# A decoder block in float32 halves on one core: low parts of the MLP's first weights, and two block sums of its second weights, made by accumulating DMA

## The chip, the cores and the metric

The kernel runs on one core of a Trainium2 chip. Time is device time in microseconds (us), from launch to end. The engines are named as in the profile: PE multiplies matrices, PEld loads its stationary operand, DVE and ACT work element by element, POOL is the general engine (GpSimd), and SP issues most DMAs. A DMA moves data between the chip's memory (HBM) and SBUF; PSUM holds the results of PE.

## The reference

One decoder block over 512 tokens of width 1024, all in float32. Only the MLP matters here:

```python
h = rms_norm(x, mlp_norm_g[i])
x = x + jnp.square(jax.nn.relu(h @ w_ff1[i])) @ w_ff2[i]
```

Here `w_ff1` is 1024 x 4096 and `w_ff2` is 4096 x 1024. In front of it stand an attention branch, a recurrent branch and their merge (`w_out`); behind it a gate with embeddings (`w_ple_gate`, `w_ple_proj`) and a last norm.

## The kernel before

**Products in halves.** Each float32 operand is split in a high part, rounded to the type fp32r, and a low part, the rest. A product is then three matmuls: high by high, high by low, low by high (`mm3`, L186, and `rows3`, L201). All weights come in units of 128 x 1024 float32 (512 KB) in `wts`. The list `seq` (L127) names the units in the order in which they are used.

**The flow of a unit.** `load_to` (L156) starts the plain load of a unit into one of two `w_raw` buffers on SP's queue. `fetch_to` (L164) then makes the parts in one of three pairs of buffers: ACT copies with rounding to `w_hi` (L175), and DVE subtracts that from the raw values to give `w_lo` (L176). `weights` (L179) hands the pair to the product. During the third step of a unit's product, `step` (L196) lets the second next unit be fetched; since there are three pairs, that fetch can't start before the unit ahead of the running one is done.

**The MLP** (from L1081). The hidden columns are taken in four groups (`qd`) of 1024. In a group, eight units of `w_ff1` (`U_FF1`) give eight tiles of 128 hidden columns by 512 tokens, 24 matmuls each. `squared` (L1126) applies ReLU and square and makes parts and sums of these tiles: `fA11`, `fA2`, `fS3`, `fS`. The second product works on 2 x 2 blocks with seven block products instead of eight (Strassen's way, in Winograd's form). The left blocks are the tiles of `squared` (`LEFT`, L1092). The right blocks are B11, B21, B12 and B22 of the group's `w_ff2`, each in two units (a, b), and sums of them. `load_block` (L1149) loads a block; `sums_early` (L1155), `T1` (L1161) and `T4` (L1164) form the sums on DVE: B12 becomes B22 - B12, T2 is that plus B11, B11 becomes B22 - T2, B21 becomes B21 - T2. `RIGHT` (L1167) names the right block of each of the seven products, `BEFORE` (L1168) the sum that is formed ahead of a unit, and `LOADS` (L1176) which blocks are loaded beside which unit of the first product. Each block is split like other weights, by `fetch_to`, since `load_to` leaves out `U_FF2`. `seventh` (L1178) runs one block product, two units of 12 matmuls each; `to_x` (L1189) adds finished sums to the residual stream `xs`.

**The order of the queues.** Each engine runs its queue in order. The framework's planner orders the queues when the program is built: by the order of the program, but what it expects to be ready may pass what it expects to wait. So the blocks of a group are loaded while the second product of the group before runs, as soon as their buffers are free, though they stand behind it in the program.

**Around it.** Ahead of the MLP `embeddings` (L1031) and `gained` (L1016) make the transposed input `hx`, `norm_of` (L1038) the norm with the scratch tile `sqj`, and `spread` (L1109) brings the norm to all partitions.

Of the kernel before, what the change touches and what calls it, by code (L numbers as in the profile page):

```python
# [10 lines left out]
F32 = mybir.dt.float32  # L11
F32R = mybir.dt.float32r
BF16 = mybir.dt.bfloat16
AF = mybir.ActivationFunctionType
ALU = mybir.AluOpType
# [3 lines left out]
P = 128  # L19
T = 512  # L20
D = 1024
# [19 lines left out]
U_PLE, U_QKV, U_RW, U_GSB, U_GRW, U_UPSB, U_UPRW, U_OUT, U_FF1, U_FF2, U_GATE = range(11)  # L41
UNITS = {U_PLE: 2, U_QKV: 12, U_RW: 14, U_GSB: 8, U_GRW: 8, U_UPSB: 4, U_UPRW: 4, U_OUT: 8, U_FF1: 32, U_FF2: 32, U_GATE: 8}
UBASE = {}
# [42 lines left out]
def tile_block(ctx: ExitStack, tc: tile.TileContext, xT, xt, pT, wts, lora, cols_d, gfin_d, consts_d, out, dbg=None):  # L86
    nc = tc.nc
    act, dve, pool, pe, sync = nc.scalar, nc.vector, nc.gpsimd, nc.tensor, nc.sync
# [3 lines left out]
    def r32(ap):  # L92
        return ap.bitcast(F32)
# [33 lines left out]
    seq = []  # L127
# [25 lines left out]
    def unit(i):  # L153
        return wts[UBASE[seq[i][0]] + seq[i][1]]

    def load_to(n):  # L156
        while len(loaded) < min(n, len(seq)):
            i = len(loaded)
            loaded.append(None)
            if seq[i][0] != U_FF2:  # L160
                loaded[i] = wpool.tile([P, 1024], F32, name="w_raw", bufs=2)
                sync.dma_start(out=loaded[i], in_=unit(i))

    def fetch_to(n, ahead=0):  # L164
        while state["i"] < min(n, len(seq)):
            i = state["i"]
            state["i"] += 1
            load_to(i + 1 + ahead)
            raw = loaded[i] if seq[i][0] != U_FF2 else sources[seq[i]]()
            if seq[i] in homes:  # L170
                hi, lo = homes[seq[i]]()
            else:
                hi = wpool.tile([P, 1024], F32R, name="w_hi")
                lo = wpool.tile([P, 1024], F32R, name="w_lo")
            act.copy(out=hi, in_=raw)  # L175
            dve.tensor_tensor(out=lo, in0=raw, in1=r32(hi), op=ALU.subtract)  # L176
            ready.setdefault(seq[i], []).append((hi, lo))

    def weights(*u):  # L179
        assert seq[state["used"]] == u, (seq[state["used"]], u)  # L180
        state["used"] += 1
        fetch_to(state["used"])
        state["due"] = 3
        return ready[u].pop(0)
# [35 lines left out]
    def split(hi, lo, src):  # L220
        act.copy(out=hi, in_=src)  # L221
        dve.tensor_tensor(out=lo, in0=src, in1=r32(hi), op=ALU.subtract)
# [13 lines left out]
    def root(r, n, v):  # L236

        vi, ri = v.bitcast(mybir.dt.int32), r.bitcast(mybir.dt.int32)
        dve.tensor_scalar(out=ri, in0=vi, scalar1=1, scalar2=None, op0=ALU.logical_shift_right)
        dve.tensor_scalar(out=ri, in0=ri, scalar1=-1.0, scalar2=float(0x5f3759df), op0=ALU.mult, op1=ALU.add)  # L240
        for _ in range(3):
            dve.tensor_tensor(out=n, in0=r, in1=r, op=ALU.mult)
            dve.scalar_tensor_tensor(out=n, in0=n, scalar=-0.5, in1=v, op0=ALU.mult, op1=ALU.mult)
            dve.scalar_tensor_tensor(out=r, in0=n, scalar=1.5, in1=r, op0=ALU.add, op1=ALU.mult)
# [27 lines left out]
    with ExitStack() as sA:  # L272
# [43 lines left out]
        with ExitStack() as s1:  # L316
# [205 lines left out]
            pss = [psm.tile([P, T], F32, name="ps_m") for _ in range(2)]  # L522
# [4 lines left out]
            for _ in islice(v, 1):  # L527
# [6 lines left out]
                              op0=ALU.mult, op1=ALU.add)  # L534
# [37 lines left out]
        with ExitStack() as s2:  # L572
# [39 lines left out]
            for hp in range(HP):  # L612
                csl = slice(hp * P, (hp + 1) * P)
                for i, (name, got) in enumerate((("w0", cum_), ("a0", a_all))):
# [3 lines left out]
                    t = p2.tile([P, T], F32, name=name, bufs=HP)  # L618
# [388 lines left out]
    def by_token(u, i, rhs, half):  # L1007

        pss = [ps_main() for _ in range(TT)]
        for kk in range(4):  # L1010
            w = weights(u, i + half * 4 + kk)
            for tt in range(TT):
                rows3(pss[tt], w, rhs, tt, kk * 2, kk == 0, kk == 3)
        return pss
# [23 lines left out]
    def norm_of(pool_, name):  # L1038

        st = pool_.tile([P, 3, TT], F32, name=name)  # L1040
        sq = pool_.tile([P, D], F32, name="sqj", tag="T2a")
        for tt in range(TT):
            act.activation(out=sq, in_=xs[:, tt, :], func=AF.Square, accum_out=st[:, 0, tt:tt + 1])
        dve.tensor_scalar(out=st[:, 0, :], in0=st[:, 0, :], scalar1=1.0 / D, scalar2=NORM_EPS, op0=ALU.mult, op1=ALU.add)
        root(st[:, 1, :], st[:, 2, :], st[:, 0, :])
        return st[:, 1, :]

    with ExitStack() as s3:
# [23 lines left out]
        for half in range(2):  # L1072
            pss = by_token(U_OUT, 0, mg, half)
# [8 lines left out]
    p4 = sM.enter_context(tc.tile_pool(name="p4", bufs=1))  # L1082
    HT = T // 2
# [13 lines left out]
    def kept(tt):  # L1097
        t = p4.tile([P, 512], F32, name="pl", tag="rk", bufs=4)
        return t

    for half in range(2):
        for tt in (half * 2, half * 2 + 1):
            t = kept(tt)
# [14 lines left out]
    def minus(out, a, b):  # L1118
        dve.tensor_tensor(out=out, in0=a, in1=b, op=ALU.subtract)  # L1119

    def plus(out, a, b):
        dve.tensor_tensor(out=out, in0=a, in1=b, op=ALU.add)

    lower = {}

    def squared(ps, m):  # L1126
        if m < 4:
            r = lower[m] = p4.tile([P, T], F32, name="rk", bufs=4)
        else:
            r = p4.tile([P, T], F32, name="r")  # L1130
        dve.scalar_tensor_tensor(out=r, in0=ps, scalar=0.0, in1=rs2, op0=ALU.max, op1=ALU.mult)
        act.activation(out=r, in_=r, func=AF.Square)
        sums = const.tile([P, 4, HT], F32, name="sums", tag="lora_w")
        lo_, hi_ = r[:, 0:HT], r[:, HT:T]
        if m < 4:
            split(fA11[0][:, m], fA11[1][:, m], lo_)
            minus(sums[:, 0], lo_, hi_)
            split(fS3[0][:, m], fS3[1][:, m], sums[:, 0])
        else:
            k, low = m - 4, lower[m - 4]  # L1140
            split(fA2[0][:, k], fA2[1][:, k], r.rearrange("p (j t) -> p j t", j=2))
            plus(sums[:, 1], low[:, HT:T], hi_)
            minus(sums[:, 2], sums[:, 1], low[:, 0:HT])
            minus(sums[:, 3], lo_, sums[:, 2])
            split(fS[0][:, k], fS[1][:, k], sums[:, 1:4])

    blocks = {}

    def load_block(qd, n, p_):  # L1149

        i = {"B11": 0, "B21": 2, "B12": 4, "B22": 6}[n] + p_
        t = blocks[n, p_] = p4.tile([P, 1024], F32, name=f"{n}{'ab'[p_]}")
        sync.dma_start(out=t, in_=wts[UBASE[U_FF2] + qd * 8 + i])

    def sums_early(p_):  # L1155

        minus(blocks["B12", p_], blocks["B22", p_], blocks["B12", p_])
        blocks["T2", p_] = p4.tile([P, 1024], F32, name=f"T2{'ab'[p_]}")
        plus(blocks["T2", p_], blocks["B12", p_], blocks["B11", p_])

    def T1(p_):  # L1161
        minus(blocks["B11", p_], blocks["B22", p_], blocks["T2", p_])

    def T4(p_):  # L1164
        minus(blocks["B21", p_], blocks["B21", p_], blocks["T2", p_])

    RIGHT = ("B11", "B21", "T2", "B11", "B12", "B22", "B21")  # L1167
    BEFORE = {4: lambda: T1(0), 5: lambda: T1(1), 7: lambda: T4(0), 8: lambda: T4(1)}  # L1168
    for qd in range(4):
        for i in range(7):  # L1170
            for p_ in range(2):
                def source(i=i, p_=p_):
                    BEFORE.get(2 * i + p_, lambda: None)()
                    return blocks[RIGHT[i], p_]
                sources[U_FF2, qd, i, p_] = source
    LOADS = [[("B12", 0), ("B22", 0)], [("B11", 0), ("B12", 1)], [("B22", 1), ("B11", 1)], [("B21", 0), ("B21", 1)]]  # L1176

    def seventh(qd, i, pss):  # L1178

# [6 lines left out]
                rows3(pss[t2], w, op, t2, p_ * 2, first and p_ == 0, p_ == 1)  # L1186
        return pss

    def to_x(pss, th, half):  # L1189
        for t2 in range(2):  # L1190
            xb = xs[:, th * 2 + t2, COLHALF[half]]
            dve.tensor_tensor(out=xb, in0=pss[t2], in1=xb, op=ALU.add)  # L1192

    for qd in range(4):
        waiting = []
        for m in range(8):
            w = weights(U_FF1, qd * 8 + m)
            for l in LOADS[m] if m < 4 else ():
                load_block(qd, l[0], l[1])
            ps = ps_main()  # L1200
            product(ps, w, hx)
            waiting.append((ps, m))
            if qd == 0 and m < 2:
                continue
            if qd == 0 and m == 2:
                spread()
            while waiting:
                squared(*waiting.pop(0))
            if m in (2, 4):
                sums_early(m // 2 - 1)  # L1210
        V = seventh(qd, 0, None)
        to_x(V, 0, 0)
        to_x(seventh(qd, 1, None), 0, 0)
        V = seventh(qd, 2, V)
        to_x(V, 0, 1)
        W = seventh(qd, 3, None)
        to_x(W, 1, 1)
        V = seventh(qd, 4, V)
        to_x(V, 1, 1)
        W = seventh(qd, 5, W)  # L1220
        to_x(W, 0, 1)
        V = seventh(qd, 6, V)
        to_x(V, 1, 0)

# [2 lines left out]
    p4 = ctx.enter_context(tc.tile_pool(name="p5", bufs=1))  # L1227
# [45 lines left out]
    pss = by_token(U_GATE, 0, hx, 0)  # L1273
# [80 lines left out]
```

## Time and profile before

| | |
|---|---|
| Time, median of 3 runs | 890.43 us (889.32 to 890.63) |
| The profiled execution's own time | 890.04 us |
| Its span, first to last instruction | 888.3 us |
| Granted clock of PE, mean | 0.997 |
| Busy share PE, PEld, DVE, ACT, POOL | 98%, 80%, 78%, 51%, 9% |
| DMA, mean over the span | 107 GB/s |

The profile shows one execution. Its rows give an engine, the line of the kernel, what is written and read, shapes, a count, and then busy time and the mean of one in ns. Windows give busy times by stretch. Waits name the engine that waited and what ended the wait. A load's landing is the time from its issue to the arrival of the last byte. A busy PE means that some matmul was in its pipeline, not that they followed as closely as they can; for that the starts in the timeline are read.

### The profile page before, as it was taken

The numbers are of one execution on the slowest core, as the hardware profiler recorded it, in microseconds if no ns is written. First come the engines' busy times: TensorE is split into PE (matmuls) and PEld (weight loads), VectorE is DVE, ScalarE is ACT, GpSimd is POOL, SyncE is SP. The second block draws the span as 40 slices with busy tenths as digits, with TensorE's granted clock in tenths as the row PEclk, the third lists the DMA queues.
The fourth block names the chain that finished last, engine by engine and source line by source line (L and its number), as shares of the span: only waits on it lengthen the run. The fifth ranks groups of instructions, "written<-read, shape, count | busy, mean of one in ns | idle before, by whom it ended". The sixth has DMA issues, their size and how long they took to land.

```text
span 888.3 us, 12491 instructions
## 1 busy us (share of the span) xinstructions
PE 871.9 (98%) x4662; PEld 706.5 (80%) x4662; DVE 689.4 (78%) x1262; ACT 456.7 (51%) x738; POOL 82.7 (9%) x137
## 2 busy tenths in 40 slices
PE   9999999999999999999999999999999999999995
PEld 5778788778787887777888888888888888888885
DVE  7899987885987968877853879867985887697766
ACT  6888887724426424443521755345434543454743
POOL 1332321001303102111000000000000000000000
PEclk9999999999999999999999999999999999999998
DMA  7322112220130223428842820542153135200422
GB/s 263 96 65 67 61 64 103 67 95 29 44 100 25 83 96 120 139 75 269 295 158 96 307 96 1 171 137 72 47 175 118 40 111 174 96 1 0 166 72 96
DMA packets 32269, 95.26 MB, mean 107 GB/s; under 512 B 3664, under 2 KB 3664, under 8 KB 32208
## 3 DMA queue, kind: packets, MB, share of 16 engines
q1 hardware_dynamic: 32208, 94.46, 31.8%
q8 instruction: 37, 0.61, 0.3%
q14 instruction: 24, 0.20, 0.1%
HBM read 83.96 MB, written 10.49 MB: 106 GB/s over the span
## 4 chain that ended last, share of the span: by engine, by line
PE 83%; DVE 9%; ACT 5%; DMA 1%; issue 1%; SPq 0%; POOL 0%; DVEq 0%; ACTq 0%
PE ps_m L191 14%; PE ps_m L192 14%; PE ps_m L193 14%; PE ps_m L208 9%; PE ps_m L207 9%; PE ps_m L206 9%; PE ps_g L809 2%; DVE w_lo L176 1%; PE ps_g L780 1%; PE ps_g L192 1%; PE ps_g L193 1%; PE ps_c L942 1%; PE ps_o L492 1%; PE ps_g L191 1%; PE ps_s L930 1%
## 5 line engine op out<-in xcount | busy, mean ns | idle before, releaser
L175 ACT CAST w_hi<-w_raw 128x1024 fp32r<-128x1024 f32 x94 | 99.2, 1055 | 152.8 <-PE ps_m L192 95.1
L176 DVE TENSOR_TENSOR w_lo<-w_raw,w_hi 128x1024 fp32r<-128x1024 f32 x94 | 115.2, 1226 | 35.5 <-ACT w_hi L175 35.2
L191 PE MATMUL ps_m<-h_hi,w_hi 128*128 128x512 f32 x320 | 129.4, 406 | 0.6 <-ACT h_hi L348 0.6
L192 PE MATMUL ps_m<-h_lo,w_hi 128*128 128x512 f32 x320 | 128.8, 402 | 0.3 <-DVE h_lo L349 0.3
L193 PE MATMUL ps_m<-h_hi,w_lo 128*128 128x512 f32 x320 | 128.6, 402 | 0.0
L191 PE MATMUL ps_m<-hx,w_hi 128*128 128x512 f32 x256 | 99.7, 390 | 0.4 <-ACT hx L1027 0.4
L192 PE MATMUL ps_m<-hx,w_hi 128*128 128x512 f32 x256 | 99.6, 390 | 0.0
L193 PE MATMUL ps_m<-hx,w_lo 128*128 128x512 f32 x256 | 99.5, 389 | 0.0
L191 PEld LDWEIGHTS ps_m<-h_hi,w_hi 128*128 128x128 f32 x320 | 60.6, 189 | 11.9 <-ACT h_hi L348 1.5
L192 PEld LDWEIGHTS ps_m<-h_lo,w_hi 128*128 128x128 f32 x320 | 60.3, 188 | 12.1 <-DVE h_lo L349 1.3
L193 PEld LDWEIGHTS ps_m<-h_hi,w_lo 128*128 128x128 f32 x320 | 60.2, 188 | 12.3
L191 PEld LDWEIGHTS ps_m<-hx,w_hi 128*128 128x128 f32 x256 | 48.0, 188 | 10.5 <-ACT hx L1027 0.6
L192 PEld LDWEIGHTS ps_m<-hx,w_hi 128*128 128x128 f32 x256 | 48.1, 188 | 10.3 <-DVE hx L1028 0.2
L193 PEld LDWEIGHTS ps_m<-hx,w_lo 128*128 128x128 f32 x256 | 48.1, 188 | 9.8
L206 PE MATMUL ps_m<-w_hi,fS 128*128 128x512 f32 x128 | 49.8, 389 | 0.0
L207 PE MATMUL ps_m<-w_lo,fS 128*128 128x512 f32 x128 | 49.8, 389 | 0.0
L208 PE MATMUL ps_m<-w_hi,fS 128*128 128x512 f32 x128 | 49.8, 389 | 0.0
L208 PE MATMUL ps_m<-w_hi,fA 128*128 128x512 f32 x96 | 37.3, 389 | 0.0
L206 PE MATMUL ps_m<-w_hi,fA 128*128 128x512 f32 x96 | 37.3, 389 | 0.0
L207 PE MATMUL ps_m<-w_lo,fA 128*128 128x512 f32 x96 | 37.3, 389 | 0.0
L221 ACT CAST fS<-sums 128x256 fp32r<-128x256 f32 (+1 forms) x32 | 19.9, 622 | 33.2 <-DVE sums L1119 33.2
L1192 DVE TENSOR_TENSOR xs<-ps_m,xs 128x512 f32<-128x512 f32 x56 | 35.9, 684 | 0.0
(379 smaller groups left out, 1942.1 us busy)
## 6 DMA issues: line engine op xcount, KB each, us to landing
w_raw<-in_wts_dram SPq DMA_DIRECT2D x98, 512.0 KB, 3.3
gates<-gg SPq DMA_DIRECT2D x16, 256.0 KB, 2.0
x_in<-in_xT_dram SPq DMA_DIRECT2D x8, 256.0 KB, 5.5
tmp<-gates SPq DMA_DIRECT2D x8, 256.0 KB, 3.2
upsb<-tmp SPq DMA_DIRECT2D x8, 256.0 KB, 3.6
ga<-upsb SPq DMA_DIRECT2D x8, 256.0 KB, 4.9
gb<-gates SPq DMA_DIRECT2D x8, 256.0 KB, 4.8
xs<-in_xt_dram SPq DMA_DIRECT2D x4, 512.0 KB, 6.0
```

Source lines behind the costliest of these rows:

```text
L175: act.copy(out=hi, in_=raw)
L176: dve.tensor_tensor(out=lo, in0=raw, in1=r32(hi), op=ALU.subtract)
L191: pe.matmul(ps, wh, xh[:, k, t], start=first, stop=False)
L192: pe.matmul(ps, wh, xl[:, k, t], start=False, stop=False)
L193: pe.matmul(ps, wl, xh[:, k, t], start=False, stop=last)
L206: pe.matmul(ps, xh[:, k + j], wh, start=first and j == 0, stop=False, skip_group_check=True)
L207: pe.matmul(ps, xh[:, k + j], wl, start=False, stop=False, skip_group_check=True)
L208: pe.matmul(ps, xl[:, k + j], wh, start=False, stop=last and j == 1, skip_group_check=True)
L221: act.copy(out=hi, in_=src)
L492: pe.matmul(ps_o[:, j * P:T], vv[:, j, hh, :, :].rearrange("p a d -> p (a d)"), part[:, ZB[j]:ZB[j] + ZN[j]], start=j == 2 and part is wh, ...
L809: pe.matmul(ps[:, k], LB[:, k, :], rhs[:, k], start=True, stop=True)
L1192: dve.tensor_tensor(out=xb, in0=pss[t2], in1=xb, op=ALU.add)
```

## The change

For units of `w_ff1` the low part isn't made by DVE any more. ACT makes a second pass over the raw values with scale -1 into `w_lo`, whose type rounds it to the negated high part, and then a DMA on POOL's queue reads the unit from HBM once more and adds it to `w_lo` in SBUF.

In the second product the signs are turned over so that every sum of blocks is a plain sum: T3 = B22 + B12 and T1 = B12 + B11, then T2 = T3 + B11 (in B11's place) and T4 = B21 + T2 (in B21's place). T3 and T1 are made by a plain load of one block and an accumulating load of the other; only T2 and T4 are formed on DVE. B11, T3, B21, T1 and B22 now have two tiles each, and B12 and T2 none: ten tiles, as before. `squared` forms its sums with other signs, and `to_x` subtracts in the right half of the columns. Loads of blocks are spread over five units of the first product instead of four. The scratch `sqj` shares T1's buffer instead of T2's.

```diff
             act.copy(out=hi, in_=raw)
-            dve.tensor_tensor(out=lo, in0=raw, in1=r32(hi), op=ALU.subtract)
+            if seq[i][0] == U_FF1:
+
+                act.activation(out=lo, in_=raw, func=AF.Copy, scale=-1.0)
+                pool.dma_start(out=lo, in_=unit(i), accum_op=ALU.add)
+            else:
+                dve.tensor_tensor(out=lo, in0=raw, in1=r32(hi), op=ALU.subtract)
...
-        sq = pool_.tile([P, D], F32, name="sqj", tag="T2a")
+        sq = pool_.tile([P, D], F32, name="sqj", tag="T1a")
...
+    def negated_minus(out, a, b):
+        dve.scalar_tensor_tensor(out=out, in0=a, scalar=-1.0, in1=b, op0=ALU.mult, op1=ALU.subtract)
...
-            plus(sums[:, 1], low[:, HT:T], hi_)
-            minus(sums[:, 2], sums[:, 1], low[:, 0:HT])
-            minus(sums[:, 3], lo_, sums[:, 2])
+            minus(sums[:, 1], hi_, low[:, HT:T])
+            negated_minus(sums[:, 2], sums[:, 1], low[:, 0:HT])
+            negated_minus(sums[:, 3], lo_, sums[:, 2])
...
-    def load_block(qd, n, p_):
-
-        i = {"B11": 0, "B21": 2, "B12": 4, "B22": 6}[n] + p_
+    BLOCK = {"B11": 0, "B21": 2, "B12": 4, "B22": 6}
+
+    def block_of(qd, n, p_):
+        return wts[UBASE[U_FF2] + qd * 8 + BLOCK[n] + p_]
+
+    def load_block(qd, n, p_, of):
+
         t = blocks[n, p_] = p4.tile([P, 1024], F32, name=f"{n}{'ab'[p_]}")
-        sync.dma_start(out=t, in_=wts[UBASE[U_FF2] + qd * 8 + i])
-
-    def sums_early(p_):
-
-        minus(blocks["B12", p_], blocks["B22", p_], blocks["B12", p_])
-        blocks["T2", p_] = p4.tile([P, 1024], F32, name=f"T2{'ab'[p_]}")
-        plus(blocks["T2", p_], blocks["B12", p_], blocks["B11", p_])
-
-    def T1(p_):
-        minus(blocks["B11", p_], blocks["B22", p_], blocks["T2", p_])
+        sync.dma_start(out=t, in_=block_of(qd, of[0], p_))
+        if len(of) > 1:
+            pool.dma_start(out=t, in_=block_of(qd, of[1], p_), accum_op=ALU.add)
+
+    def T2(p_):
+
+        plus(blocks["B11", p_], blocks["T3", p_], blocks["B11", p_])
 
     def T4(p_):
-        minus(blocks["B21", p_], blocks["B21", p_], blocks["T2", p_])
-
-    RIGHT = ("B11", "B21", "T2", "B11", "B12", "B22", "B21")
-    BEFORE = {4: lambda: T1(0), 5: lambda: T1(1), 7: lambda: T4(0), 8: lambda: T4(1)}
+
+        plus(blocks["B21", p_], blocks["B21", p_], blocks["B11", p_])
+
+    RIGHT = ("B11", "B21", "B11", "T1", "T3", "B22", "B21")
+    BEFORE = {4: lambda: T2(0), 5: lambda: T2(1), 7: lambda: T4(0), 8: lambda: T4(1)}
...
-    LOADS = [[("B12", 0), ("B22", 0)], [("B11", 0), ("B12", 1)], [("B22", 1), ("B11", 1)], [("B21", 0), ("B21", 1)]]
+    LOADS = [[(n, p_, of) for p_ in range(2)] for n, of in
+             (("B11", ("B11",)), ("T3", ("B22", "B12")), ("B21", ("B21",)), ("T1", ("B12", "B11")), ("B22", ("B22",)))]
...
-    def to_x(pss, th, half):
+    def to_x(pss, th, half, op=ALU.add):
...
-            dve.tensor_tensor(out=xb, in0=pss[t2], in1=xb, op=ALU.add)
+            dve.tensor_tensor(out=xb, in0=xb, in1=pss[t2], op=op)
...
-            for l in LOADS[m] if m < 4 else ():
-                load_block(qd, l[0], l[1])
+            for l in LOADS[m] if m < 5 else ():
+                load_block(qd, *l)
...
-            if m in (2, 4):
-                sums_early(m // 2 - 1)
+
```

More of the change, by code (lines that the diff above doesn't have):

```diff
@@ L1214, in tile_block @@
         V = seventh(qd, 2, V)
-        to_x(V, 0, 1)
+        to_x(V, 0, 1, ALU.subtract)
         W = seventh(qd, 3, None)
-        to_x(W, 1, 1)
+        to_x(W, 1, 1, ALU.subtract)
         V = seventh(qd, 4, V)
-        to_x(V, 1, 1)
+        to_x(V, 1, 1, ALU.subtract)
         W = seventh(qd, 5, W)
-        to_x(W, 0, 1)
+        to_x(W, 0, 1, ALU.subtract)
         V = seventh(qd, 6, V)
```

## The prediction

> **What bounds the kernel now.** I read the windows first, cut at the two ends of the MLP, then what TensorE waited for inside it. The columns of a window are its bounds, its length, the busy time of PE, PEld, DVE, ACT and POOL with the number of instructions, the granted clock, the DMA share and the GB/s.
>
> ```profile
> 498.00:826.00 328.00, 327.98 (x1450) 271.39 (x1451) 258.36 (x358) 149.38 (x194) 0.00 (x0) 1.00 0.30 98
> ```
>
> ```profile
> PE ps_m L191 <- ACT hx L1027: 0.4, 1, 0.4
> ```
>
> The MLP is 328 us long, PE is busy for 327.98 of them at the full clock, and the second row, the whole list of PE's waits in it, is one wait of 0.4 us for ACT. A busy PE can hide pipelining, so I looked at how its matmuls follow each other, in the timeline around the start of the third group of 1024 hidden columns (start, length, engine, line, operation).
>
> ```profile
> 657.18 0.39 PE L206 MATMUL ps_m<-w_hi,fA 128*128 128x512 f32 x1
> 657.40 0.39 PE L207 MATMUL ps_m<-w_lo,fA 128*128 128x512 f32 x1
> ...
> 659.90 0.39 PE L206 MATMUL ps_m<-w_hi,fA 128*128 128x512 f32 x1
> ...
> 662.62 0.39 PE L191 MATMUL ps_m<-hx,w_hi 128*128 128x512 f32 x1
> 662.85 0.39 PE L192 MATMUL ps_m<-hx,w_hi 128*128 128x512 f32 x1
> 663.07 0.39 PE L193 MATMUL ps_m<-hx,w_lo 128*128 128x512 f32 x1
> ```
>
> The 24 matmuls from 657.18 to 662.62 start 5.44/24 = 0.2267 us apart, with no step at the border between the second and the first weights. So one first-weight unit (24 matmuls) lasts 5.44 us and one second-weight unit (12) 2.72 us. All 4 x 360 = 1440 matmuls of the MLP need 1440 x 0.2267 = 326.4 us, and the stretch has 328. The whole slack of the MLP is 1.5 us, and part of that is real work (the small products of `spread`). **A change that only takes work off DVE can gain at most these 1.5 us here; what it can do is make PE late.** So I price the relief at nothing and look at what becomes due later.
>
> **What is removed.** DVE's idle time costs nothing, so its relief is counted only to show that it is off the path.
>
> ```profile
> L176 DVE TENSOR_TENSOR w_lo<-w_raw,w_hi 128x1024 fp32r<-128x1024 f32 x32 | 39.1, 1223 | 5.4 <-ACT w_hi L175 5.3
> L1119 DVE TENSOR_TENSOR B12a<-B22a,B12a 128x1024 f32<-128x1024 f32 x4 | 4.9, 1219 | 1.0 <-DMA B22a<-in_wts_dram 1.0
> ```
>
> 32 low parts of 1.22 us go, 39 us. Of the eight block sums of a group (two tiles each of B12, T2, T1 and T4) four remain, so 4 x 4 x 1.22 = 19.5 us go. DVE falls from 258 to about 200 us of 328. PE waits for none of it: value 0. The turned signs exchange one operation on 128x256 for another, 0.42 us each by the rows of `sums`, on an engine with more idle time: 0. `negated_minus`, `to_x` with its operands exchanged and the new tag of `sqj` go with them: 0.
>
> **What is added on ACT.** One more pass over 128x1024 for each first-weight unit.
>
> ```profile
> L175 ACT CAST w_hi<-w_raw 128x1024 fp32r<-128x1024 f32 x32 | 33.9, 1058 | 65.8 <-PE ps_m L192 45.5 <-PE ps_m L208 13.3 <-DMA w_raw<-in_wts_dram 6.9
> ```
>
> 32 x 1.06 = 34 us on an engine that is busy for 149 of 328: hidden as a sum. Queued behind the pass stand the squares and splits of `squared`; their results are first read in the second product, units later. The place where ACT has no room is the start.
>
> ```profile
> 486.00:498.00 12.00, 11.63 (x68) 9.76 (x66) 7.69 (x14) 9.44 (x21) 0.00 (x0) 1.00 0.79 282
> 501.01 1.13 ACT L175 CAST w_hi<-w_raw 128x1024 fp32r<-128x1024 f32 x1
> ```
>
> Here the norm's squares (`sqj`), which nobody needs until `spread`, can step back, so the pass costs PE between 0 and its own 1.06 us.
>
> **What is added by DMA.** Each group gets 8 accumulating loads for first weights, 4 for T3 and T1, and 2 more plain loads: 14 x 0.524 x 4 = 29.4 MB on top of 94.5.
>
> ```profile
> q1 hardware_dynamic: 32208, 94.46, 31.8%
> ```
>
> That is 10% of the engines' time more, and 8% again if an accumulating load also has to read its target (25 MB): some 50% in all. No queue is full on average. What counts is the **latency** of one low part. T1 and T3 have time: as the plain loads do now, they start in the second products of the group before, and their first reader is more than 30 us later. On POOL's queue they stand ahead of the first weights' accumulation, but should be done by then.
>
> In the middle of a first product there is also room.
>
> ```profile
> 668.03 1.05 ACT L175 CAST w_hi<-w_raw 128x1024 fp32r<-128x1024 f32 x1 [2.82 <-PE ps_m L192]
> 668.99 0.62 ACT L1132 ACTIVATE rk<-rk 128x512 f32<-128x512 f32 x1
> 669.65 0.41 ACT L221 CAST fA<-rk 128x256 fp32r<-128x256 f32 x1
> 671.05 0.41 ACT L221 CAST fS<-sums 128x256 fp32r<-128x256 f32 x1 [0.99 <-DVE sums L1119]
> ```
>
> The cast of unit 3 starts at 668.03, when unit 0 gives its buffer back. The new pass ends at 670.1 if it goes first, at 671.1 if it goes into the idle 0.99 us. Unit 3's third matmul (the first to read the low part) is due at 663.07 + 3 x 5.44 = 679.4. So the DMA has 8.3 to 9.3 us.
>
> The tight place is the **first unit of groups two, three and four**, because the units ahead of it last only 2.72 us.
>
> ```profile
> 657.38 1.06 ACT L175 CAST w_hi<-w_raw 128x1024 fp32r<-128x1024 f32 x1 [1.67 <-PE ps_m L208]
> 660.10 1.06 ACT L175 CAST w_hi<-w_raw 128x1024 fp32r<-128x1024 f32 x1 [1.66 <-PE ps_m L208]
> 659.51 1.22 DVE L176 TENSOR_TENSOR w_lo<-w_raw,w_hi 128x1024 fp32r<-128x1024 f32 x1
> ```
>
> Cast at 657.38, now low part on DVE done at 660.73, 2.3 us ahead of 663.07. After the change: cast to 658.4, negated pass to 659.4 (an ACT instruction starts 0.1 us before the end of the one before), then the DMA. It has 663.07 - 659.42 = **3.65 us**.
>
> No accumulating load stands in the trace, so I bound it by the plain loads of the same 512 KB.
>
> ```profile
> DMA to landing us min/median/max: 3.1/3.2/3.5
> DMA to landing us min/median/max: 3.3/3.4/7.4
> cols<-in_cols_dram SPq DMA_DIRECT2D x1, 37.0 KB, 1.8
> 660.75 31.71 SPq L162 DMA_DIRECT2D w_raw<-in_wts_dram  x8
> ```
>
> The rows are w_raw from 650 to 700 us, B21a, the smallest load, and the issue of w_raw. Low end 3.1 us (the read of the target costs nothing, POOL issues as fast as SP): in time. High end 7.4 us, the longest landing, where loads stood behind each other: 3.75 us late. I take 3.2 for the plain load, plus 3.2 - 1.8 = 1.4 for a second read of as many bytes, plus 0.7, half a transfer, because the next w_raw starts at the same moment (its buffer, as now at 660.75, is given back by the last reader, which is now the new ACT pass): **5.3 us, so 1.65 us late**. The second unit's pass ends at 662.2 and its third matmul is due at 663.07 + 5.44 = 668.5: 6.3 us, in time.
>
> [...]
>
> In the first group the third unit is exposed: cast at 501.01, pass done at 503.1 or later, due near 498.4 + 10.9 + 0.45 = 509.7, so 6.6 us, while more loads than now crowd the same microseconds. With ACT's stretch together: 0 to 3, I take 0.5.
>
> **Sum**, against the profiled execution's own 890.04 (span 888.3, 1.74 around it; the median of the runs shown is 0.4 higher): 890.04 + 3 x 1.65 + 0.5 = **895.5 us**, three late starts, half a microsecond at the beginning, and nothing gained.
>
> **The rivals.**
>
> A, not slower: the low part is in time, or PE doesn't notice. For it speaks that the planner of PE's queue does move products past each other where it expects an operand late; at the first unit of all it did.
>
> ```profile
> 498.88 0.39 PE L193 MATMUL ps_m<-hx,w_lo 128*128 128x512 f32 x1
> 499.11 0.40 PE L192 MATMUL ps_m<-hx,w_hi 128*128 128x512 f32 x1
> 499.34 0.40 PE L191 MATMUL ps_m<-hx,w_hi 128*128 128x512 f32 x1
> 499.58 0.39 PE L193 MATMUL ps_m<-hx,w_lo 128*128 128x512 f32 x1
> ```
>
> In program order each trio is L191, L192, L193; here the third trio's L191 stands ahead of the second's L193. If it plans the accumulating load as long as it is, it puts the 16 products with the high part first, and 14 x 0.2267 = 3.2 us of them cover the 1.65. Against it: a DMA that takes longer than planned isn't covered, and the queue was planned without these collisions. It decides at a DMA of 3.65 us, or at a plan that is right within 0.6 us a start. Time: 890.0 + 0 to 1.8, some 890.6.
>
> B, my forecast: 1 to 4 us at each of the three starts and 0 to 3 in the first group, 893 to 905, likeliest 895.5.
>
> C, the accumulating load is far slower than two reads (POOL writes descriptors slowly, or the adding stage is narrow). From 8.3 to 9.3 us on, the middle of the first product is late too: three buffers tie unit 3 to the end of unit 0, so each us beyond some 8.8 costs a third of it per unit. At 10 us: 3 x (10 - 3.65) = 19 at the starts and 29 units x 1.2/3 = 12: 31 us, 921. Beyond 5.44 us of pure transfer the DMA engines themselves would set the pace, and it is worse. Against it: nothing in a plain load's 3.2 us points to such a factor.
>
> D, faster: DVE's relief pulls the 1.5 us of slack in, and the order of the queues falls luckily at the start: 888.4. For it speaks only that the 0.4 us wait lies where DVE and ACT are fuller than elsewhere.
>
> That the change doesn't take the low parts off DVE can't be: it is written out. But the accumulation could be served in another order on POOL's queue, T3 and T1 ahead of the first weights; in the first group, where all of them start together, that is in the 0 to 3.
>
> **How the numbers follow.** A 0.37, B 0.43, C 0.15, D 0.05. The point is that of B, 895.5. The range reaches down to D's side of no change, 888.9, and up into C as far as the 7.4 us of the longest load allow with the first group's 3 us and one more unit late in each group: 890.4 + 3 x 3.75 + 3 + 3 x 2 = 911. It leaves out most of C and a little of D. Differences under 0.2%, 1.8 us, can't be told from no change. Faster by more: D, 0.05. Within: A, 0.37. Slower: B and C, 0.58.
>
> **What would show it.** The issue of the accumulating loads on POOL's queue with their time to landing: about 5.3 us for w_lo, where 3.65 or less means A and over 8 means C. In PE's waits: w_lo at L193, three times some 1.65 us, at the first unit of the second to fourth group. In PE's timeline there: trios in order (B), or many L191 and L192 ahead of the first L193 (A). ACT's second pass right behind the cast, 1.06 us. DVE near 200 us in the MLP and the DMA share near 0.5, without effect on the span. The forecast is wrong if PE's queue was planned around the load, if POOL takes microseconds to issue one, or if the loads of a unit queue behind those of the blocks.

## The result, and the profile after

| | before | after |
|---|---|---|
| Time, median | 890.53 us (889.32 to 890.72) | 925.16 us (923.1 to 926.27) |
| The profiled execution's own time | 890.04 us | 923.1 us |
| Its span | 888.3 us | 921.0 us |
| Ratio after to before | | 1.0389, 95% interval 1.0369 to 1.0410 |

The change costs 34.6 us. The direction and the place were forecast, the size was not: 895.5 us, with a range up to 911.

The window of the profile after with the same bounds as the first one of the prediction (same columns):

```profile
498.00:826.00 328.00, 303.93 (x1309) 249.11 (x1308) 183.65 (x286) 165.14 (x215) 39.72 (x46) 0.96 0.74 186
```

PE had 327.98 busy us here and has 303.93. The granted clock has fallen from 1.00 to 0.96, and the DMA share has risen from 0.30 to 0.74. PE's list of waits in the profile after names what it waited for (total, times, longest, in us); its first row is:

```profile
PE ps_m L198 <- DMA w_lo<-in_wts_dram: 24.0, 4, 9.3
```

This is one new wait, four times, for the low part of a first-weight unit (L198 is the L193 of before). It stands at the third unit of the first group and at the first unit of the other three. The timeline of PE at the start of the second group, after:

```profile
592.78 0.39 PE L196 MATMUL ps_m<-hx,w_hi 128*128 128x512 f32 x1
593.01 0.39 PE L197 MATMUL ps_m<-hx,w_hi 128*128 128x512 f32 x1
598.36 0.73 PE L198 MATMUL ps_m<-hx,w_lo 128*128 128x512 f32 x1 [4.96 <-DMA w_lo<-in_wts_dram]
598.88 0.63 PE L196 MATMUL ps_m<-hx,w_hi 128*128 128x512 f32 x1
599.31 0.63 PE L197 MATMUL ps_m<-hx,w_hi 128*128 128x512 f32 x1
...
602.35 0.40 PE L196 MATMUL ps_m<-hx,w_hi 128*128 128x512 f32 x1
602.58 0.39 PE L197 MATMUL ps_m<-hx,w_hi 128*128 128x512 f32 x1
```

Two things are to be read here. The third matmul, due 0.23 us after 593.01, starts at 598.36: 5.12 us late. And the matmuls behind it start 0.43 us apart (598.88 to 599.31), although they wait for nothing; from 602.35 on they are 0.23 apart again. The windows around this place show what that is (same columns as above):

```profile
587.00:592.00 5.00, 5.00 (x24) 4.14 (x23) 1.70 (x4) 3.96 (x4) 1.47 (x2) 1.00 1.06 280
593.00:598.40 5.40, 0.44 (x3) 0.04 (x1) 0.67 (x1) 0.00 (x0) 0.00 (x0) 1.00 1.07 279
598.00:602.00 4.00, 3.64 (x9) 2.90 (x10) 0.00 (x0) 1.23 (x2) 0.00 (x0) 0.57 0.83 225
602.00:640.00 38.00, 38.00 (x169) 31.43 (x168) 17.89 (x32) 22.79 (x33) 5.18 (x6) 1.00 0.78 167
```

After the wait the granted clock is 0.57 for four microseconds and then 1.00. And ahead of the start, while PE still works at full speed, the 16 DMA engines are full (a share of 1.06). The groups of DMA issues between 564 and 600 us show who fills them (count, KB each, median us to landing):

```profile
w_lo<-in_wts_dram POOLq DMA_DIRECT2D x2, 512.0 KB, 10.2
w_raw<-in_wts_dram SPq DMA_DIRECT2D x2, 512.0 KB, 11.1
B11a<-in_wts_dram SPq DMA_DIRECT2D x1, 512.0 KB, 3.3
...
T1a<-in_wts_dram POOLq DMA_DIRECT2D x1, 512.0 KB, 8.9
T3a<-in_wts_dram SPq DMA_DIRECT2D x1, 512.0 KB, 7.9
...
T3b<-in_wts_dram POOLq DMA_DIRECT2D x1, 512.0 KB, 8.6
B21b<-in_wts_dram SPq DMA_DIRECT2D x1, 512.0 KB, 9.7
```

The first block still lands in 3.3 us. From the first accumulation (T1a on POOL) on, every load takes 7.4 to 11 us, plain loads too: the blocks of the next group queue up in the engines, and the two low parts that the next product needs first stand at the end of this queue.

From the page of the profile after, over the whole execution:

```profile
q1 hardware_dynamic: 33360, 98.66, 32.2%
q0 software_dynamic: 6912, 25.17, 14.7%
...
L198 PE MATMUL ps_m<-hx,w_lo 128*128 128x512 f32 x256 | 103.2, 403 | 24.0 <-DMA w_lo<-in_wts_dram 24.0
...
L179 POOL DMA_DIRECT2D w_lo<-in_wts_dram x32 | 28.1, 879 | 210.2 <-ACT w_lo L178 210.2
...
L178 ACT ACTIVATE w_lo<-w_raw 128x1024 fp32r<-128x1024 f32 x32 | 33.8, 1058 | 41.6 <-DMA w_raw<-in_wts_dram 27.5
...
w_raw<-in_wts_dram SPq DMA_DIRECT2D x98, 512.0 KB, 3.6
w_lo<-in_wts_dram POOLq DMA_DIRECT2D x32, 512.0 KB, 7.7
```

An accumulating load takes 7.7 us in the median, twice a plain one, and 0.88 us of POOL to issue. Per byte its queue costs the DMA engines 14.7 / 25.17 against 32.2 / 98.66, a factor of 1.79.

**Where the 34 us went, as a sum.** All steps between the starts of PE's matmuls from 498 to 859 us, by when the MLP of the slowest kernel has ended, fall into three sorts: some 0.227 us, some 0.43 us, and waits above 0.65 us. Waits less 0.227 each: 9.41 + 5.12 + 4.84 + 5.27 = 24.6 us. The other steps above 0.3 us: 36 more than before, 7.4 us in all. Together 32.0 of the 32.7 us by which the span grew. DVE's relief does not appear in it.

The same two terms, taken from the timeline of every experiment below, account for its span too:

| run | waits | slow steps | sum | span less 888.3 |
|---|---|---|---|---|
| after | 24.6 | 7.4 | 32.0 | 32.7 |
| e1_blocks_only | 2.3 | 0 | 2.3 | 2.2 |
| e2_lows_only | 12.8 | 9.0 | 21.9 | 22.2 |
| e3_starts_dve | 13.1 | 5.5 | 18.5 | 18.5 |
| e4_waiters_dve | 17.9 | 7.6 | 25.6 | 25.0 |
| e5_pool_no_add | 12.4 | 3.3 | 15.7 | 15.1 |
| e6_high_first | 14.1 | 7.6 | 21.6 | 23.9 |
| e7_pe_kept_busy | 10.3 | 3.6 | 13.9, and 13.6 of added matmuls | 27.7 |
| e8_lows_not_first | 0 | 0 | 0 | 0.5 |
| e9_lows_high_first | 0 | 0.4 | 0.4 | 0.4 |

The rows agree within 0.7 us. Only e6 leaves 2.3 us; its list of waits has one of 2.1 us for `h_hi`, ahead of the MLP, in a part that no edit touches.

### The profile page after: what moved, and what is told of

It reads as the page before. It is cut to its first block, busy times and chain, and to the rows that moved or that the text cites. A ratio compares the mean times of both kernels' runs of the same rounds, so it can differ in the third digit from the quotient of the medians.

```text
span 921.0 us, 12650 instructions
## 1 busy us (share of the span) xinstructions
PE 880.0 (96%) x4662; PEld 710.7 (77%) x4662; DVE 636.5 (69%) x1214; ACT 485.7 (53%) x770; POOL 124.1 (13%) x185
## 3 DMA queue, kind: packets, MB, share of 16 engines
q1 hardware_dynamic: 33360, 98.66, 32.2%
q0 software_dynamic: 6912, 25.17, 14.7%
## 4 chain that ended last, share of the span: by engine, by line
PE 75%; DMA 10%; DVE 8%; ACT 4%; issue 2%; POOL 0%; SPq 0%; POOLq 0%; ACTq 0%; DVEq 0%
PE ps_m L198 14%; PE ps_m L196 13%; PE ps_m L197 13%; PE ps_m L211 6%; PE ps_m L212 6%; PE ps_m L213 6%; DMA w_lo<-in_wts_dram 5%; DMA T3b<-in_wts_dram 3%; PE ps_g L814 2%; DVE w_lo L181 1%; PE ps_g L785 1%; PE ps_o L497 1%; ACT w_hi L175 1%; PE ps_c L947 1%; PE ps_z L505 1%
## 5 line engine op out<-in xcount | busy, mean ns | idle before, releaser
L198 PE MATMUL ps_m<-h_hi,w_lo 128*128 128x512 f32 x320 | 128.6, 402 | 0.0
L198 PE MATMUL ps_m<-hx,w_lo 128*128 128x512 f32 x256 | 103.2, 403 | 24.0 <-DMA w_lo<-in_wts_dram 24.0
L196 PE MATMUL ps_m<-hx,w_hi 128*128 128x512 f32 x256 | 102.4, 401 | 0.1
L197 PE MATMUL ps_m<-hx,w_hi 128*128 128x512 f32 x256 | 102.3, 400 | 0.0
L181 DVE TENSOR_TENSOR w_lo<-w_raw,w_hi 128x1024 fp32r<-128x1024 f32 x62 | 76.0, 1226 | 27.4 <-ACT w_hi L175 27.2
L198 PEld LDWEIGHTS ps_m<-hx,w_lo 128*128 128x128 f32 x256 | 49.8, 194 | 36.4 <-DMA w_lo<-in_wts_dram 26.0
L196 PEld LDWEIGHTS ps_m<-h_hi,w_hi 128*128 128x128 f32 x320 | 60.5, 189 | 12.8 <-ACT h_hi L353 1.7
L198 PEld LDWEIGHTS ps_m<-h_hi,w_lo 128*128 128x128 f32 x320 | 60.2, 188 | 12.3
L197 PEld LDWEIGHTS ps_m<-hx,w_hi 128*128 128x128 f32 x256 | 49.7, 194 | 10.8 <-DVE hx L1033 0.2
L196 PEld LDWEIGHTS ps_m<-hx,w_hi 128*128 128x128 f32 x256 | 49.7, 195 | 10.7 <-ACT hx L1032 0.3
L179 POOL DMA_DIRECT2D w_lo<-in_wts_dram x32 | 28.1, 879 | 210.2 <-ACT w_lo L178 210.2
L178 ACT ACTIVATE w_lo<-w_raw 128x1024 fp32r<-128x1024 f32 x32 | 33.8, 1058 | 41.6 <-DMA w_raw<-in_wts_dram 27.5
L213 PE MATMUL ps_m<-w_hi,fS 128*128 128x512 f32 x128 | 49.8, 389 | 0.0
L212 PE MATMUL ps_m<-w_lo,fS 128*128 128x512 f32 x128 | 49.8, 389 | 0.0
L1141 DVE SCALAR_TENSOR_TENSOR rk<-ps_m,rs 128x512 f32<-128x512 f32 x16 | 10.9, 689 | 51.9 <-PE ps_m L198 50.4
L1204 DVE TENSOR_TENSOR xs<-xs,ps_m 128x512 f32<-128x512 f32 x56 | 36.0, 679 | 11.9 <-PE ps_m L213 11.9
L213 PE MATMUL ps_m<-w_hi,fA 128*128 128x512 f32 x96 | 37.4, 389 | 0.0
```

The lines of the kernel that those rows point to most:

```text
L178: act.activation(out=lo, in_=raw, func=AF.Copy, scale=-1.0)
L179: pool.dma_start(out=lo, in_=unit(i), accum_op=ALU.add)
L196: pe.matmul(ps, wh, xh[:, k, t], start=first, stop=False)
L197: pe.matmul(ps, wh, xl[:, k, t], start=False, stop=False)
L198: pe.matmul(ps, wl, xh[:, k, t], start=False, stop=last)
L212: pe.matmul(ps, xh[:, k + j], wl, start=False, stop=False, skip_group_check=True)
```

## The experiments

The theory after the result: the accumulating load is slower by itself than forecast, T1 and T3 crowd the engines where the next group begins, and every long wait costs PE some more at a low clock. The rivals: one of the first two alone explains all; the slow products come from the crowded memory and not from the wait; the middle of the first products is late as well (C of the prediction).

**e1_blocks_only: T3 and T1 by DMA, low parts on DVE as before.** Against the kernel after:

```diff
-            if seq[i][0] == U_FF1:
+            if False:
```

> The low parts of the first weights are made by DVE again; T3 and T1 stay with the accumulating DMA. Theory W (all of the 34 us are four waits of PE for a low part of the first weights at the start of a group, and the slow clock after them): no such low part comes by DMA, the blocks are due more than 30 us after their loads, so 890.5 us within 2, and no wait of PE above 0.5 us. Rival L (the DMA engines are simply loaded too heavily, whoever issues): the blocks' 8 more plain and 16 accumulating loads still crowd the same microseconds, raw weights come late, 897 us or more.

Measured: 892.24 us, ratio 1.0025 (1.0014 to 1.0035). The waits of PE that its list adds in the MLP:

```profile
PE ps_m L212 <- DVE w_lo L181: 1.0, 2, 0.5
...
PE ps_m L1120 <- DVE dg L1119: 0.7, 1, 0.7
```

They are three short waits for DVE in the first group, and none for a DMA. The accumulating loads of the blocks cost 2 us when nothing urgent stands behind them. Crowding alone is not the cause.

**e2_lows_only: the kernel before with the first part of the diff alone**, low parts by DMA, all block sums on DVE:

```diff
+            if seq[i][0] == U_FF1:
+
+                act.activation(out=lo, in_=raw, func=AF.Copy, scale=-1.0)
+                pool.dma_start(out=lo, in_=unit(i), accum_op=ALU.add)
+            else:
+                dve.tensor_tensor(out=lo, in0=raw, in1=r32(hi), op=ALU.subtract)
```

> The other half alone: block sums on DVE as before the change, the first weights' low parts by accumulating DMA. Theory W with the latency of the accumulating load itself as its main part (7.6 us in the middle of a group, where 3.65 are allowed at its start): 4 us late at three starts, 0 to 2 us of slow clock after each, 0 to 5 in the first group: 903 to 915 us. If crowding by the blocks' loads is the main part, the load takes some 5 us here and the time is 890 to 897.

Measured: 912.23 us, a single run. Its waits, and the start of its second group on ACT, POOL and PE:

```profile
PE ps_m L198 <- DMA w_lo<-in_wts_dram: 12.2, 4, 3.4
```

```profile
580.78 1.06 ACT L178 ACTIVATE w_lo<-w_raw 128x1024 fp32r<-128x1024 f32 x1 [1.44 <-PE ps_m L212]
581.75 1.04 ACT L175 CAST w_hi<-w_raw 128x1024 fp32r<-128x1024 f32 x1
```

```profile
582.13 0.86 POOL L179 DMA_DIRECT2D w_lo<-in_wts_dram  x1 [47.14 <-ACT w_lo L178]
```

```profile
586.47 0.39 PE L197 MATMUL ps_m<-hx,w_hi 128*128 128x512 f32 x1
590.18 0.79 PE L198 MATMUL ps_m<-hx,w_lo 128*128 128x512 f32 x1 [3.32 <-DMA w_lo<-in_wts_dram]
```

The load is issued at 582.13 and due at 586.47 + 0.23 = 586.70, so it has 4.57 us, not 3.65: the negated pass stands ahead of the cast here. Its row shows it released by L212, the last reader of the old low part, while L213 behind it still reads the old high part; why the planner chose this order is not shown. PE starts at 590.18, when the load has landed, 8.0 us after its issue. The window ahead of that issue and the one that ends with PE's wait, in e2 (same columns):

```profile
575.00:582.00 7.00, 7.00 (x33) 5.79 (x32) 7.00 (x9) 3.32 (x4) 0.00 (x0) 1.00 0.51 164
582.00:586.50 4.50, 4.50 (x22) 3.70 (x20) 3.19 (x5) 2.78 (x3) 1.73 (x2) 1.00 0.89 220
```

The engines are half idle until the load starts; what it meets then is the next weight load beside it and the second accumulation. So the load's own latency, with this company, costs four waits of some 3.2 us and the slow steps behind them: two thirds of the whole loss.

**e5_pool_no_add: the loads on POOL's queue overwrite their target.** This kernel leaves the additions out; sizes, queues and order are those of the kernel after.

```diff
-                pool.dma_start(out=lo, in_=unit(i), accum_op=ALU.add)
+                pool.dma_start(out=lo, in_=unit(i))
...
-            pool.dma_start(out=t, in_=block_of(qd, of[1], p_), accum_op=ALU.add)
+            pool.dma_start(out=t, in_=block_of(qd, of[1], p_))
```

> As the changed kernel, but the loads on POOL's queue overwrite their target and add nothing: the additions that make w_lo, T3 and T1 are left out, all transfers and their order stay. If the adding (the second read) is what makes such a load 7.6 us long, it lands after 4 to 5 us here (3.2 of a plain load, 0.5 more to issue on POOL, a neighbour), PE's waits at the starts fall from 5.1 to 0.5 to 2 us and the time is 892 to 903. If POOL's queue is what makes it long, it still takes 7 us or more and the time stays above 912.

Measured: 905.54 us, a single run. From its page:

```profile
q0 software_dynamic: 6912, 25.17, 8.1%
...
L179 POOL DMA_DIRECT2D w_lo<-in_wts_dram x32 | 17.2, 537 | 214.5 <-ACT w_lo L178 214.4
...
w_lo<-in_wts_dram POOLq DMA_DIRECT2D x32, 512.0 KB, 4.7
```

The same bytes take 8.1% of the engines instead of 14.7%, the landing falls from 7.7 to 4.7 us, and the issue from 0.88 to 0.54 us. So it is the adding that makes the load long: 3.0 us between the medians, of which 0.34 lie on POOL. The time came out a little above what was expected, as steps of 2.1 to 5.2 us remain at the four places. There even a load that adds nothing is late: it has some 4.6 us (e2), its median is 4.7, and at the start of the second group it took 7.1, as the engines are fuller there than the median load finds them. The window of e5 ahead of the start of its second group (same columns):

```profile
582.00:587.00 5.00, 5.00 (x24) 4.14 (x23) 1.14 (x2) 3.44 (x4) 1.06 (x2) 1.00 0.93 325
```

**e8_lows_not_first: e2 with the first units on DVE.** In the first group the first five, in the others the first two keep DVE's low part; the other 21 come by DMA.

```diff
-            if seq[i][0] == U_FF1:
+            if seq[i][0] == U_FF1 and seq[i][1] % 8 >= (5 if seq[i][1] < 8 else 2):
```

> Block sums on DVE; low parts by accumulating DMA, but not those of the first five units of the first group and of the first two of the others. It tells whether the third and later units are late by an accumulating load's own 7.6 us or only where the blocks' loads crowd it. By its own latency against the 8.3 to 9.3 us that a unit in the middle allows: no wait, 890 to 892 us. Rival C of the prediction (too slow for the middle by itself): above 898.

Measured: 890.22 us, ratio 1.0008 (0.9998 to 1.0018). No wait for a low part is left, though a load still takes as long:

```profile
w_lo<-in_wts_dram POOLq DMA_DIRECT2D x21, 512.0 KB, 7.6
```

The middle of a first product has 8.3 us or more, and 7.6 fit. Rival C, the middle late by itself, falls.

**e3_starts_dve: the same condition in the kernel after**, so that T1 and T3 come by DMA too.

> As the changed kernel, but the low parts of the first five units of the first group and of the first two of the other groups are made by DVE; 21 of 32 stay with the accumulating DMA. Theory W: no wait is left, 890.5 to 892 us. Rival C of the prediction (an accumulating load is too slow for the middle of the product too): still above 900.

Measured: 911.86 us (four runs from 908.54 to 916.72, the profiled one the shortest), ratio 1.0264 (1.0222 to 1.0307): a plain miss. The waits were not removed but moved to the first units that still come by DMA, in the first group to the second of them. ACT's waits for raw weights in the MLP, in e3 and then in e8:

```profile
ACT w_hi L175 <- DMA w_raw<-in_wts_dram: 31.0, 6, 8.1
```

```profile
ACT w_hi L175 <- DMA w_raw<-in_wts_dram: 5.9, 3, 2.1
```

The two kernels differ only in the block sums (with the change of signs that goes with them). With T1 and T3 in the queue the raw weights come late, then ACT's passes, then the accumulations. So crowding, which cost 2 us of span in e1, costs 18 us (906.8 against 888.8) as soon as low parts in the same microseconds need the same engines. The two causes don't add up: each alone leaves some room, both together none.

**e4_waiters_dve: only the four units that were waited for on DVE** (`seq[i][1] not in (2, 8, 16, 24)` in the same condition).

> As the changed kernel, but only the four low parts for which PE waited (unit 2 of the first group, unit 0 of the other three) are made by DVE. Theory W with others late in their shadow: the next unit's low part lands some 10 us after its issue and is then due after 6 to 8, so PE waits for it instead, 2 to 4 us at three places and up to 8 in the first group, 897 to 910 us. If those four alone are late: 891.

Measured: 915.02 us, a single run, above the range that was expected. Its waits:

```profile
PE ps_m L198 <- DMA w_lo<-in_wts_dram: 16.6, 8, 5.4
```

Eight waits instead of four: the units behind had been late as well, hidden in the shadow of the first. That is why a list of waits doesn't tell what their removal is worth.

**e7_pe_kept_busy: 20 matmuls into a spare tile ahead of the first unit of groups two to four**, so that PE doesn't stand still while the load is late.

```diff
+            if qd > 0 and m == 0:
+                spare = ps_main()
+                for _ in range(20):
+                    pe.matmul(spare, w[0][:, 0:P], hx[0][:, 0, :], start=True, stop=True)
```

> As the changed kernel, with 20 extra matmuls (4.5 us, result unread) ahead of the first unit of groups two to four, in the time in which PE waits anyway. If the products behind each wait run at 0.427 us instead of 0.227 because PE stood idle (the granted clock falls), they run at 0.227 here behind the three starts and the time falls by 2 us a start, to about 919. If they are slow for another reason (the crowd of DMAs), the spacing behind the waits stays 0.427 and the time is 925 or more.

Measured: 919.27 us, ratio 1.0336 (1.0318 to 1.0354), some 5 us less than the kernel after by the spans (916.0 against 921.0), although 60 matmuls (13.6 us) were added. Two windows of PE alone (busy, granted clock, DMA share, GB/s), the first behind the untouched wait of group one, the second behind the start of group two:

```profile
520.00:524.00 4.00, 4.00 (x11) 0.50 1.06 277
598.00:602.00 4.00, 3.83 (x18) 1.00 0.78 215
```

The low clock is gone where PE was kept at work and stays where it wasn't; in the kernel after the second window had 0.57 at a DMA share of 0.83. So the slow products come from PE's idle time and not from the crowded memory. In the table the slow steps fall from 7.4 to 3.6 us, and all steps of 0.427 us that are left lie behind the wait of group one. In the kernel after, seven or eight of them stood behind each of the three starts, 0.2 us longer each: some 1.5 us a start.

**e6_high_first: in each first-weight unit the 16 products with the high part go ahead of the 8 with the low part** (the kernel after otherwise).

```diff
+        if high_first:
+            for k in range(nk):
+                wh = w[0][:, k * P:(k + 1) * P]
+                pe.matmul(ps, wh, rhs[0][:, k, t], start=k == 0, stop=False)
+                pe.matmul(ps, wh, rhs[1][:, k, t], start=False, stop=False)
+                step()
+            for k in range(nk):
+                pe.matmul(ps, w[1][:, k * P:(k + 1) * P], rhs[0][:, k, t], start=False, stop=k == nk - 1)
+            return
```

> As the changed kernel, but in each unit of the first product all 16 matmuls with the high part stand ahead of the 8 with the low part. Theory W: each low part is due 14 x 0.2267 = 3.2 us later, so the waits fall from 5.1 to 1.9 us in three groups and from 9.4 to 6.2 in the first, and the short ones leave the clock alone: 898 to 907 us. If low parts are late by the rate of the loads and not by their latency, the lateness only moves: above 915.

Measured: 914.05 us, a single run: a miss. The steps at the starts of groups two to four fell from 5.35, 5.06 and 5.50 to 2.75, 2.19 and 2.57 us, but each was still followed by some eight slow steps, so that only the waits became cheaper and the term of the clock stayed. The landing went up besides:

```profile
w_lo<-in_wts_dram POOLq DMA_DIRECT2D x32, 512.0 KB, 8.1
```

**e9_lows_high_first: e2 with the same order of products.** The miss of e6 had left open whether late loads can be covered at all, or whether the crowd follows PE.

> Block sums on DVE as before, all 32 low parts by accumulating DMA (as in e2_lows_only), and in every first-weight unit the 16 products with the high part ahead of the 8 with the low part. The first product with a low part of a unit is then due 14 x 0.227 = 3.2 us later. In e2_lows_only the gaps at the four exposed units were 3.1 to 3.7 us. Theory (the load's own latency against its due time): the gaps shrink to 0 to 0.6 us each, too short for a lower granted clock, so both the waits and the products at 0.427 us go: 890.5 to 893 us, waits for w_lo under 2.5 us in all. Rival (the lateness of these units is crowding that follows PE's own progress, as the miss of e6_high_first would have it): loads are late again by 2 to 3 us each and the slow products remain: 903 to 912 us.

Measured: 891.36 us, ratio 1.0011 (1.0001 to 1.0020). From its page:

```profile
L224 PE MATMUL ps_m<-hx,w_lo 128*128 128x512 f32 x256 | 63.5, 390 | 0.0
...
w_lo<-in_wts_dram POOLq DMA_DIRECT2D x32, 512.0 KB, 7.6
```

All 32 accumulating loads are there, as slow as ever, and PE waits for none of them. A due time 14 x 0.227 = 3.2 us later covers waits of 2.9 to 3.5 us almost to the end, and the low clock goes with them. That settles the first cause: it is latency against due time. It also shows what DVE's relief is worth: 32 low parts are off DVE (224.76 busy us in the window from 498 to 826, where before had 258.36), PE is fed in time, and the kernel is no faster than before.

## Why the prediction was right or wrong

**What bounds the kernel, and the value of DVE's relief: right.** PE was the bound with some 1.6 us of slack (328 less 326.4; the prediction writes 1.5). In e8 and e9 DVE has less to do and the time is that of before, within 0.1%.

**Removed work: right.** DVE fell by 52.9 us over the span, from 689.4 to 636.5; 39 + 19.5 = 58.5 were forecast. Added up one by one, its instructions do fall by that much (59.7 us); some of them overlap a little in the trace, so the busy time falls by less. Nothing hung on it. **ACT's second pass: right in size** (1.058 us) and hidden. Its place at the starts of groups two to four was not foreseen: it goes ahead of the cast, so the load had 4.57 us at e2's second group instead of 3.65. This error was in the change's favour.

**The place: right.** PE waited for w_lo at the first unit of groups two to four, in program order; the trios were not moved past each other (rival A), and the middle of the products was in time in e8 (rival C), whose 921 us came near by another way. By the prediction's own sign (over 8 us for `w_lo` means C) the 9.4 to 9.8 us at the three starts of the kernel after would have spoken for C; e8 shows that they hold for the starts and not for the middle.

**The step that failed is the 5.3 us.** "I take 3.2 for the plain load, plus 3.2 - 1.8 = 1.4 for a second read of as many bytes, plus 0.7, half a transfer": these 5.3 us measured 8.0 us at the start of e2's second group and 7.6 to 7.8 in the medians of e2, e8 and e9. On POOL's queue a load without the addition, beside its neighbour and in the traffic of e5, took 4.7 where 3.2 + 0.7 = 3.9 stood, and the addition took 3.0 where 1.4 stood. At e2's three starts PE was late by 3.48, 2.86 and 2.98 us, 9.3 together, where 3 x 1.65 = 5 stood.

That the addition costs a second read of as many bytes was the author's estimate; no run shows such a read. In the engines' time the same bytes cost 1.85 times as much with it (14.7% of 921.0 us against 8.1% of 903.4), and the load at e2's second group took 2.7 us longer than the 5.3 of the estimate.

**That T1 and T3, ahead of the first weights' accumulation on POOL's queue, "should be done by then" failed.** The prediction names this among the signs of being wrong. POOL's queue at the start of the second group, after:

```profile
585.90 0.86 POOL L1168 DMA_DIRECT2D T3b<-in_wts_dram  x1 [3.01 <-DMA T3b<-in_wts_dram]
588.68 0.86 POOL L179 DMA_DIRECT2D w_lo<-in_wts_dram  x1 [1.92 <-ACT w_lo L178]
```

T3b's accumulation, which takes 8.6 us to land, was issued only 2.8 us ahead of w_lo and was still under way. "No queue is full on average" was true of the span (32.2 + 14.7 = 47% of the engines, some 50% were forecast) and misleading: nearly all of the added time falls into the MLP, a good third of the span, where the share is 0.74 and ahead of each start 1.05. With it the lateness at the three starts rises from 3.1 to 5.1 us each (e2 against after).

**The first group, "0 to 3, I take 0.5", failed worst**: 9.4 us. The forecast itself named the cause, loads that crowd the same microseconds and POOL's order, and then priced it at next to nothing. The window of the kernel after shows the size:

```profile
509.90:519.40 9.50, 0.27 (x2) 0.00 (x0) 0.00 (x0) 2.00 (x2) 1.59 (x2) 0.67 1.05 275
```

PE has 0.27 busy us of 9.50, and the engines are full throughout. The load that it waits for was issued late as well:

```profile
505.83 1.21 POOL L179 DMA_DIRECT2D w_lo<-in_wts_dram  x1
```

It was due at 509.78 + 0.23 = 510.01, so it had 4.2 us and not the 6.6 of the prediction, and it took 13.6: the negated pass started only at 503.78, behind a square of the norm, and POOL issued T3b's accumulation first, at 505.29. With blocks taken off the DMA path (e2) the step at this place was 3.7 us.

**A term was missing altogether:** the granted clock behind each long wait, 7.4 us in the kernel after. The prediction's own first window shows a clock of 1.00, but in it PE never stood still (327.98 busy us of 328).

So the forecast 3 x 1.65 + 0.5 = 5.5 us stands against 15.2 at the three starts, 9.4 in the first group and 7.4 of slow steps. The upper end of the range took the longest plain load, 7.4 us, as the worst that an accumulating load could do; in the crowd those that PE waited for took 9.4 to 13.6.

What stays open: how much of the 8.0 us in e2 is the second weight load that starts beside it. No run put an accumulating load alone. The nearest is one in e2 at 522.16 us, which shared its time with one plain load of 3.1 us and still took 7.5; by this the company is worth some half a microsecond, an estimate.

## What to carry to other kernels

Before a computation is moved from an idle engine to a DMA, ask for the shortest distance between the moment when its inputs are there and the first reader, and price the DMA at its latency there, with an accumulating load at about twice the plain one (7.7 against 3.6 us in the kernel after). Take the share of the DMA engines from the stretch in which the transfers fall, not from the span, and see what stands in front of the urgent one. A wait of PE can cost more than its length (7.4 us of slow steps behind four waits in the kernel after, 9.0 behind four in e2), and if a transfer must be late, work that doesn't need it belongs ahead of it, until the rest of the wait is short.

## What the runs showed of the hardware that was not expected

**Behind long waits PE ran at half clock for a while.** Behind the four waits of the kernel after, the products started 0.427 instead of 0.227 us apart for 3.5 to 4.0 us, at a granted clock of 0.50 (for example from 598.46 to 601.88 us). In all timelines of the MLP, every step of 3.6 us or more between two starts was followed by such slow products. No step of 2.11 us or less was. Between these, most were (2.19 and 2.75 us in e6, 2.45 in e4, 3.09 and 3.21 in e2) and two weren't, 2.79 us in e5 and this one in e4:

```profile
685.87 0.39 PE L197 MATMUL ps_m<-hx,w_hi 128*128 128x512 f32 x1
689.14 0.50 PE L198 MATMUL ps_m<-hx,w_lo 128*128 128x512 f32 x1 [2.88 <-DMA w_lo<-in_wts_dram]
689.47 0.39 PE L196 MATMUL ps_m<-hx,w_hi 128*128 128x512 f32 x1
689.70 0.40 PE L197 MATMUL ps_m<-hx,w_hi 128*128 128x512 f32 x1
```

A wait of 3.27 us from start to start, and full speed at once.

The granted clock of the kernel after was 0.50 in four stretches of the MLP: from 513.13 to 523.37, 598.46 to 601.88, 687.21 to 690.62 and 772.54 to 779.37 us. They last 10.24, 3.41, 3.41 and 6.83 us, and all their beginnings and ends lie whole multiples of 3.41 us apart. What separates the waits that were followed by slow products from the two that weren't is not shown: their lengths alone don't (2.19 us in e6 was enough, 3.27 in e4 wasn't), and no run shifted a wait while its length stayed.

**Adding costs at three places**: POOL's issue (0.88 against 0.54 us, and 0.33 on SP), the engines' time (1.85 times for the same bytes), and the landing (7.7 against 4.7 us).
